# A transformer block in fp32 on one core: both column pairs of the output projection by seven products for eight

## The chip, the cores and the metric

The kernel runs on one core of a Trainium2 chip. The metric is the device time of one execution in microseconds. Its engines work in parallel and wait for each other on semaphores: TensorE (PE, with its weight loads PEld), VectorE (DVE), ScalarE (ACT), GpSimd (POOL) and SyncE (SP), which here issues most of the loads. POOL issues the other DMAs.

## The reference

One residual block over 512 tokens of width 2048, eight stick-breaking heads and eight latent-attention heads, 128 wide each. Cut to what matters here:

```python
h = rms_norm(x, pre_norm_w); proj = h @ w_in
o_a = stick_breaking_attention(sb_q, sb_k, sb_v)            # 8 heads x 128
o_b = chunk_causal_softmax_attention(q_mla, k_mla, v_mla)   # 8 heads x 128
mixed = concatenate([o_a * silu(sb_gate), o_b * silu(mla_gate)])   # 512 x 2048
y = mixed @ w_out                                           # 2048 x 2048
return x + rms_norm(y, post_norm_w)
```

## The kernel before

Every fp32 product is made of three matmuls: each operand is split into a high part (a cast on ScalarE) and a low part (a subtract on VectorE, `split`), and `mm3` adds hi x hi, hi x lo and lo x hi. So each weight tile of 128x1024 (`raw`, loaded by SP) passes ScalarE (`whi`) and VectorE (`wlo`) before TensorE reads it; four raw and three split tiles are in flight.

TensorE never runs attention alone. A generator, `filler()`, yields steps of three matmuls of the big projections in a fixed order: the latent projection, the gates, then for each stick-breaking head q, k and its gate (v of four heads at once, ahead of heads 0 and 4), and last the output projection. The attention code takes such steps between its own matmuls with `fill(n)`, and `need(key)` runs steps until a projection is done. The latent heads come first; the loop over the eight stick-breaking heads h follows, and what is left of the filler, which is the output projection, runs at the end.

A head's result (`mix`, 128 features x 512 tokens) is put into DRAM (`mixed`). For the output projection the kernel loads it again (`mx`) and splits it.

The 2048 output columns are four groups of 512. Groups 0 and 1 go the plain way (`out_group`): 16 feature chunks x 4 token blocks x 3 matmuls each. Groups 2 and 3 are one pair in `last_columns`: features in two halves, tokens in two halves, columns in two halves make a 2x2 block product, which is done with seven half-size products (A11, S1, S2, S3, A22, S4, A12) instead of eight. Its operands are sums of blocks: sums of weights (`w_sums`) and sums of mixed (s1, s2 and s4, `first_sums`; s3, `late_sums`). The weights' sums are made during the heads: `load_weight_parts(j)` loads four 128x512 pieces by POOL into "wsum" tiles, `weight_sums(j)` subtracts on VectorE and stores the results to DRAM by POOL, and the products load them as weights. Each product is 4 weight tiles x 2 chunks x 2 token blocks x 3 matmuls. Sums of the products are added on VectorE (`s1`, `s15`), `sum_piece` makes `y`, its sum of squares and the weighted `y`. The last product is done token block by token block (`kept` weights), and `residual` ends each block.

Tiles come from tagged pools, and a tile waits until its slot is free: "qrt" has 8 slots, "mv" 4, "tr" 4, "g" 48. Instructions marked `keep_in_program_order` keep their order on an engine; the others are placed by the scheduler. The matmuls, SP's loads and the wsum subtracts are marked.

Of the kernel before, what the change touches and what calls it, by code (L numbers as in the profile page):

```python
# [19 lines left out]
P = 128  # L20
S = 512
# [36 lines left out]
def block(ctx: ExitStack, tc: tile.TileContext, a: dict):  # L58
# [317 lines left out]

    order = list(range(H, 2 * H)) + list(range(H))
    msplit = []
    last_mixed = {}

    def split_mixed():
        n = len(msplit)
        if n == 2 * H:
            return
        i = order[n]
        tag = "qrt" if n < 4 else "g"
        hi, lo = g(f"mxh{i}", F32R, tag), g(f"mxl{i}", F32R, tag)
        if i == H - 1:
            mx = last_mixed[0]
        else:  # L390
            mx = g("mx", tag="mv")
            pool.dma_start(out=mx, in_=mixed[i])
        split(hi, lo, mx)
        msplit.append((hi, lo))

    def out_mm(ps, b, c, wh, wl):
        mh, ml = msplit[c]
        mm3(ps, tokens(mh, b), tokens(ml, b), wh, wl, c == 0, c == 15)

    ssy = [const.tile([P, 5], F32, name=f"ssy{b}") for b in range(NB)]  # L400
    ypw = [{} for _ in range(NB)]
    y_tags = iter(["q4"] * 4 + ["row"] * 6 + ["gt"] * 2 + ["g"] * 5)
# [30 lines left out]
    def out_group(gi):  # L433
        banks = [bank(f"y{b}") for b in range(NB)]
        for i in range(8):
            wh, wl = weights(a["w_o"][gi, i], 1024)
            if i == 0:
                for _ in range(4):
                    split_mixed()
            at = 8 * gi + i - 6  # L440
            if 0 <= at + 1 < H:
                load_pair(at + 1)
            if 0 <= at < H:
                first_sums(at)
            for j in range(2):
                s_ = slice(j * S, (j + 1) * S)
                split_mixed()
                for b in range(NB):
                    out_mm(banks[b], b, i * 2 + j, wh[:, s_], wl[:, s_])
                    yield  # L450
        pw = post_weight(gi)
        for b in range(NB):
            out_piece(b, gi * S, banks[b], pw)

# [3 lines left out]
    sums = {}  # L458
    w_sums = [dram.tile([4, P, 1024], F32, name=f"w_sums{n}") for n in range(4)]

    w_parts = {}

    def load_weight_parts(j):
        i, c = j // 2, slice((j % 2) * S, (j % 2 + 1) * S)
        w_parts[j] = []
        for gi, k in ((2, 0), (3, 0), (3, 4), (2, 4)):
            t = g("wsum", tag="qrt")
            tc.keep_in_program_order(pool.dma_start(out=t, in_=a["w_o"][gi, k + i][:, c]))
            w_parts[j].append(t)

    def weight_sums(j):

        i, c = j // 2, slice((j % 2) * S, (j % 2 + 1) * S)
        b11, b12, b22, b21 = w_parts.pop(j)
        for n, (out, x, y) in ((0, (b11, b12, b11)), (2, (b12, b22, b12)), (1, (b22, b22, b11)), (3, (b21, b21, b22))):
            tc.keep_in_program_order(dve.tensor_tensor(out=out, in0=x, in1=y, op=ALU.subtract))
            tc.keep_in_program_order(pool.dma_start(out=w_sums[n][i][:, c], in_=out))

    def mixed_again(n):
        t = g("mx", tag="mv")  # L480
        pool.dma_start(out=t, in_=mixed[order[n]])
        return t

    pairs = {}

    def load_pair(j):
        pairs[j] = mixed_again(j), mixed_again(j + 8)

    def first_sums(j):

        x, y = pairs.pop(j)
        t, s4 = g("st", tag="tr"), g("st4", tag="tr")[:, :HALF]
# [4 lines left out]
        h12, l12, hl4 = g("s12h", F32R), g("s12l", F32R), g("s4", F32R)  # L497
        split(h12, l12, t)
# [514 lines left out]
```

## Time and profile before

| | |
|---|---|
| median of 3 runs | 852.88 us (852.85 to 853.16) |
| the profiled execution | 851.63 us, its span 849.9 us |
| mean granted clock of TensorE, share of full | 0.998 |
| matmuls in the profile | 4050 |
| busy: PE, PEld, DVE, ACT, POOL | 98%, 82%, 57%, 43%, 11% of the span |
| moved by DMA | 126.84 MB |

The profile is of one execution; the span runs from its first instruction to its last. Busy time of an engine is a mean over stretches of different kinds, so stretches are read apart. A row of a timeline gives the start, the length, the engine, the line, output<-inputs, and in brackets how long the engine idled before and what ended it.

### The profile page before, as it was taken

To read this page: it belongs to the slowest core of one execution; us is meant where nothing else is said; L and a number is where in the kernel's file an instruction comes from. 1 tells how busy PE (TensorE), PEld (TensorE's weight loads), DVE (VectorE), ACT (ScalarE), POOL (GpSimd) and SP (SyncE) were. 2 spreads that over 40 slices of the span, in tenths; PEclk is the share of its full clock that TensorE was granted. 3 is DMA by queue.
4 is the path that set the end of the run, shared out by engine and by line. 5 is a ranking of instruction groups with operands and counts; after the bars stand their busy time and mean duration, and the time that the engine had idled before them with its cause. 6 is when DMAs were issued, how large, how long until landed. Compare 5 with 4: busy or idle time off the path is not lost.

```text
span 849.9 us, 10987 instructions
## 1 busy us (share of the span) xinstructions
PE 834.2 (98%) x4050; PEld 700.0 (82%) x4050; DVE 484.5 (57%) x866; ACT 361.6 (43%) x620; POOL 90.2 (11%) x189
## 2 busy tenths in 40 slices
PE   8999999999999999999999999999999999999995
PEld 5889988888888888888888888888878888888884
DVE  5676765556665533647374623555574768435876
ACT  7742655545555323334242413333342535324641
POOL 1000000000000040111111010111120122100001
PEclk9999999999999999999999999999999999999999
DMA  9823222222221164434434342425362556525984
GB/s 333 342 81 106 100 81 81 81 94 81 81 90 65 63 223 161 146 99 164 161 124 154 131 140 97 145 91 199 131 222 98 179 176 222 162 99 182 324 305 155
DMA packets 41909, 126.84 MB, mean 149 GB/s; under 512 B 5808, under 2 KB 6080, under 8 KB 41856
## 3 DMA queue, kind: packets, MB, share of 16 engines
q1 hardware_dynamic: 29952, 88.62, 30.0%
q0 software_dynamic: 10608, 35.42, 12.6%
q10 hardware_dynamic: 1296, 2.11, 0.7%
q8 instruction: 32, 0.52, 0.3%
q14 instruction: 21, 0.17, 0.1%
HBM read 109.34 MB, written 16.78 MB: 148 GB/s over the span
## 4 chain that ended last, share of the span: by engine, by line
PE 87%; DMA 4%; DVE 3%; issue 3%; ACT 1%; POOL 1%; SPq 0%; DVEq 0%; POOLq 0%; ACTq 0%
PE gps L122 19%; PE v L122 10%; PE qp L122 10%; PE kp L122 9%; PE y L122 6%; PE cq L122 4%; PE av L122 4%; PE mz L122 3%; DMA mx<-mixed 3%; PE mqp L122 3%; PE sx L122 3%; PE sz L122 3%; PE ckv L122 2%; PE sv L122 2%; PE tp L125 2%
## 5 line engine op out<-in xcount | busy, mean ns | idle before, releaser
L99 DVE TENSOR_TENSOR wlo<-raw,whi 128x1024 fp32r<-128x1024 f32 (+2 forms) x137 | 163.2, 1191 | 138.6 <-ACT whi L96 137.1
L96 ACT CAST whi<-raw 128x1024 fp32r<-128x1024 f32 (+2 forms) x137 | 140.6, 1026 | 212.5 <-PE v L122 43.5
L122 PE MATMUL gps<-hh,whi 128*128 128x512 f32 x256 | 102.0, 398 | 0.0
L122 PE MATMUL gps<-hl,whi 128*128 128x512 f32 x256 | 100.1, 391 | 0.0
L122 PE MATMUL gps<-hh,wlo 128*128 128x512 f32 x256 | 99.9, 390 | 0.0
L122 PEld LDWEIGHTS gps<-hh,wlo 128*128 128x128 f32 x256 | 48.1, 188 | 10.6
L99 DVE TENSOR_TENSOR tl<-tp,th 128x512 fp32r<-128x512 f32 (+1 forms) x64 | 31.1, 486 | 42.4 <-ACT th L96 42.0
L96 ACT CAST th<-tp 128x512 fp32r<-128x512 f32 (+1 forms) x64 | 27.1, 424 | 66.2 <-PE tp L125 66.0
L122 PEld LDWEIGHTS gps<-hl,whi 128*128 128x128 f32 x256 | 48.3, 189 | 7.6
L122 PEld LDWEIGHTS gps<-hh,whi 128*128 128x128 f32 x256 | 48.2, 188 | 7.6
L122 PE MATMUL qp<-hh,whi 128*128 128x512 f32 x128 | 52.1, 407 | 0.0
L122 PE MATMUL v<-whi,hh 128*128 128x512 f32 x128 | 50.9, 397 | 0.0
L122 PE MATMUL y<-whi,mxh 128*128 128x512 f32 x128 | 50.3, 393 | 0.2 <-DVE y L416 0.2
L122 PE MATMUL qp<-hh,wlo 128*128 128x512 f32 x128 | 50.1, 391 | 0.0
L122 PE MATMUL qp<-hl,whi 128*128 128x512 f32 x128 | 50.0, 391 | 0.0
L122 PE MATMUL v<-whi,hl 128*128 128x512 f32 x128 | 49.9, 390 | 0.0
L122 PE MATMUL v<-wlo,hh 128*128 128x512 f32 x128 | 49.9, 390 | 0.0
L122 PE MATMUL y<-whi,mxl 128*128 128x512 f32 x128 | 49.9, 390 | 0.0
L122 PE MATMUL y<-wlo,mxh 128*128 128x512 f32 x128 | 49.9, 389 | 0.0
L122 PE MATMUL kp<-hh,whi 128*128 128x512 f32 x128 | 49.8, 389 | 0.0
L122 PE MATMUL kp<-hl,whi 128*128 128x512 f32 x128 | 49.8, 389 | 0.0
L122 PE MATMUL kp<-hh,wlo 128*128 128x512 f32 x128 | 49.8, 389 | 0.0
(296 smaller groups left out, 1790.6 us busy)
## 6 DMA issues: line engine op xcount, KB each, us to landing
raw<-in_w_t SPq DMA_DIRECT2D x64, 512.0 KB, 3.3
raw<-in_w_o SPq DMA_DIRECT2D x24, 512.0 KB, 3.3
mx<-mixed POOLq DMA_DIRECT2D x39, 256.0 KB, 3.5
raw<-in_w_v SPq DMA_DIRECT2D x16, 512.0 KB, 3.2
wsum<-in_w_o POOLq DMA_DIRECT2D x32, 256.0 KB, 5.2
w_sums<-wsum POOLq DMA_DIRECT2D x32, 256.0 KB, 2.6
raw<-w_sums SPq DMA_DIRECT2D x16, 512.0 KB, 3.4
xs<-in_x SPq DMA_DIRECT2D x16, 256.0 KB, 6.3
```

The costliest lines, as they stand in the source:

```text
L96: i = act.copy(out=hi, in_=src)
L99: dve.tensor_tensor(out=lo, in0=src, in1=hi.bitcast(F32), op=ALU.subtract)
L122: tc.keep_in_program_order(pe.matmul(out=out, lhsT=lhsT, rhs=rhs, start=start, stop=stop, **kw))
L125: tc.keep_in_program_order(pe.transpose(out, in_, identity))
```

## The change

Both column pairs now go by seven products: `out_columns(u)` for u = 0 (groups 0, 1) and u = 1 (groups 2, 3), in the order A11, S3, S1, S2, S4, A22, A12. `out_group`, `split_mixed`, `first_sums` and `late_sums` are gone.

The weights' sums are made for both pairs, 64 loads and 64 stores instead of 32 and 32. `w_todo` says which eighths belong to which head: two to heads 0 and 4, one to heads 1, 2, 3 and 5. The loads of a head's first eighth (eight at once) are issued in the head before; the sums of pair 0 come before the head's scores, those of pair 1 after them.

The mixed operands' sums are made once for both pairs. `head_sums` makes s1, s2 and s4 behind every head and stores them to DRAM. `latent_parts` loads and splits the latent halves with s3 in place (k1), four in head 6 and four ahead of head 7's scores. `other_parts` loads s12, s4 and the stick-breaking halves (k2) beside the first pair's products A11, S3, S1, S2 and S4, three loads ahead, through the four "mv" slots. The second pair finds all of them split already.

Pinned splits keep their subtract in program order too. Scores of heads 0 to 6 have `fill(6)` ahead, not `fill(4)`. In the tail the second piece instead of the third goes by ScalarE and POOL.

```diff
     def split(hi, lo, src, scale=None, pin=False):
         if scale is None:
             i = act.copy(out=hi, in_=src)
+            j = dve.tensor_tensor(out=lo, in0=src, in1=hi.bitcast(F32), op=ALU.subtract)
             if pin:
                 tc.keep_in_program_order(i)
-            dve.tensor_tensor(out=lo, in0=src, in1=hi.bitcast(F32), op=ALU.subtract)
+                tc.keep_in_program_order(j)
         else:
...
+    w_sums = [[dram.tile([4, P, 1024], F32, name=f"w_sums{u}_{n}") for n in range(4)] for u in range(2)]
+    a_sums = [(dram.tile([P, S], F32, name=f"s12_{j}"), dram.tile([P, HALF], F32, name=f"s4_{j}")) for j in range(H)]
-    def load_weight_parts(j):
+    def load_weight_parts(u, j):
...
+        for gi, k in ((0, 0), (1, 0), (1, 4), (0, 4)):
             t = g("wsum", tag="qrt")
-            tc.keep_in_program_order(pool.dma_start(out=t, in_=a["w_o"][gi, k + i][:, c]))
...
-    def weight_sums(j):
+            tc.keep_in_program_order(pool.dma_start(out=t, in_=a["w_o"][2 * u + gi, k + i][:, c]))
+            w_parts[u, j].append(t)
+    def weight_sums(u, j):
...
-        b11, b12, b22, b21 = w_parts.pop(j)
+        b11, b12, b22, b21 = w_parts.pop((u, j))
         for n, (out, x, y) in ((0, (b11, b12, b11)), (2, (b12, b22, b12)), (1, (b22, b22, b11)), (3, (b21, b21, b22))):
             tc.keep_in_program_order(dve.tensor_tensor(out=out, in0=x, in1=y, op=ALU.subtract))
-            tc.keep_in_program_order(pool.dma_start(out=w_sums[n][i][:, c], in_=out))
-
-    def mixed_again(n):
-        t = g("mx", tag="mv")
-        pool.dma_start(out=t, in_=mixed[order[n]])
+            tc.keep_in_program_order(pool.dma_start(out=w_sums[u][n][i][:, c], in_=out))
+    def from_dram(src, w=S):
+        t = g("mx", tag="mv")[:, :w]
+        pool.dma_start(out=t, in_=src)
         return t
...
+    def head_sums(h, x, y):
+        t, s4 = g("st", tag="mv"), g("st4", tag="mv")[:, :HALF]
         s1, s2 = t[:, :HALF], t[:, HALF:]
         dve.tensor_tensor(out=s1, in0=x[:, HALF:], in1=y[:, HALF:], op=ALU.add)
         dve.tensor_tensor(out=s2, in0=s1, in1=x[:, :HALF], op=ALU.subtract)
         dve.tensor_tensor(out=s4, in0=y[:, :HALF], in1=s2, op=ALU.subtract)
+        pool.dma_start(out=a_sums[h][0], in_=t)
+        pool.dma_start(out=a_sums[h][1], in_=s4)
+    k1, s12, k2, s4s = [], [], [], []
+    def latent_parts(js, tag, steps=2):
+        xs = []
+        for j in js:
+            x = from_dram(mixed[H + j])
+            xs.append(x)
+        for x in xs:
+            fill(steps)
+            tc.keep_in_program_order(dve.tensor_tensor(out=x[:, HALF:], in0=x[:, :HALF], in1=x[:, HALF:], op=ALU.subtract))
+            hi, lo = g("k1h", F32R, tag), g("k1l", F32R, tag)
+            split(hi, lo, x, pin=True)
+            k1.append((hi, lo))
+    def other_parts():
+        srcs = [(a_sums[j][0], S) for j in range(H)] + [(a_sums[j][1], HALF) for j in range(H)] + [(mixed[j], S) for j in range(H)]
+        ahead = [from_dram(*srcs[n]) for n in range(3)]
+        for n in range(3 * H):
+            x = ahead.pop(0)
+            if H <= n < 2 * H:
+                hl4 = g("s4", F32R)
+                split(hl4[:, :HALF], hl4[:, HALF:], x, pin=True)
+                s4s.append(hl4)
+            else:
+                hi, lo = g("kh", F32R), g("kl", F32R)
+                split(hi, lo, x, pin=True)
+                (s12 if n < H else k2).append((hi, lo))
+            if n + 3 < 3 * H:
+                ahead.append(from_dram(*srcs[n + 3]))
+            if n < H or n >= 2 * H or n % 2:
+                yield
...
+    def out_columns(u):
+        w11, w21, w22 = ([a["w_o"][2 * u + gi, k + i] for i in range(4)] for gi, k in ((0, 0), (0, 4), (1, 4)))
+        t1, t2, t3, t4 = w_sums[u]
+        at = (2 * u * S, (2 * u + 1) * S)
+        parts = other_parts() if u == 0 else iter(())
         x = [bank("sx") for _ in range(2)]
+        yield from product(x, "A11", w11, True, False, parts)
         s1 = [g("s1", tag="t") for _ in range(2)]
         s15 = [g("s15", tag="t") for _ in range(2)]
         for r in range(2):
             act.copy(out=s1[r], in_=x[r])
+        v = [bank("sv") for _ in range(2)]
+        yield from product(v, "S3", t3, True, False, parts)
         z = [zbank("sz") for _ in range(2)]
+        beside = parts if u == 0 else keep_weights()
+        yield from product(z, "S1", t1, True, True, beside)
         for r in range(2):
             dve.tensor_tensor(out=s15[r], in0=z[r], in1=s1[r], op=ALU.add)
         y = [tbank("sy") for _ in range(2)]
+        yield from product(y, "S2", t2, True, True, beside)
         for r in range(2):
             dve.tensor_tensor(out=s1[r], in0=y[r], in1=s1[r], op=ALU.add)
             dve.tensor_tensor(out=s15[r], in0=y[r], in1=s15[r], op=ALU.add)
+        pws = [post_weight(2 * u), post_weight(2 * u + 1)]
         junk = g("junk", tag="tr")
         for r in range(2):
+            sum_piece(2 + r, at[1], v[r], s15[r], pws[1], junk)
+        z = [zbank("sz") for _ in range(2)]
+        yield from product(z, "S4", w22, True, True, parts if u == 0 else load_x(2))
         for r in range(2):
+            sum_piece(r, at[1], z[r], s15[r], pws[1], junk)
+        yield from product(v, "A22", t4, False, True, iter(()) if u == 0 else load_x(0))
         for r in range(2):
+            sum_piece(2 + r, at[0], v[r], s1[r], pws[0], junk)
+        if u == 0:
+            yield from product(x, "A12", w21, False, True)
+            for r in range(2):
+                out_piece(r, at[0], x[r], pws[0], junk)
+            return
         for b in (2, 3):
             residual(b)
         for b in (0, 1):
             for j in range(8):
                 mm3(x[b], *factor("A12", j, b), *kept[j], False, j == 7, skip_group_check=True)
                 yield
+            out_piece(b, at[0], x[b], pws[0], junk)
             residual(b, b == 1)
...
-            if tail and i == 2:
+            if tail and i == 1:
...
-        for gi in range(2):
-            yield from out_group(gi)
-        yield from last_columns()
+        for u in range(2):
+            yield from out_columns(u)
...
@@ -917,17 +881,30 @@
         fill(max(0, 4 * NK + NK * (h + 2) - taken[0]))
 
-    load_weight_parts(H - 1)
+    def load_parts(j):
+        for u in range(2):
+            load_weight_parts(u, j)
+    w_todo = {0: [0, 1], 1: [2], 2: [3], 3: [4], 4: [5, 6], 5: [7]}
+    load_parts(0)
     for h in range(H):
-        if h == 0:
-            fill(8)
-            weight_sums(H - 1)
+        late = None
+        for n, j in enumerate(w_todo.get(h, ())):
+            if n:
+                weight_sums(1, late)
+                load_parts(j)
+                fill(30)
+            else:
+                fill(10)
+            weight_sums(0, j)
+            late = j
+        if h == H - 1:
+            latent_parts(range(4, 8), "g")
         kh, kl = need("k", h)
         qh, ql = need("q", h)
-        fill(4)
+        fill(6 if h < H - 1 else 4)
         rows = row_tiles("beta")
-        if h < H - 1:
-            load_weight_parts(h)
+        x = from_dram(mixed[H + h])
         for b in range(NB):
             n = (b + 1) * P
             w = max(n, 256)
@@ -941,17 +918,20 @@
                                    initial=1.0, op0=ALU.mult, op1=ALU.add)
             dve.tensor_tensor(out=beta[:, :n - 1], in0=beta[:, :n - 1], in1=prod[:, 1:n], op=ALU.mult)
             fill((1, 3, 3, 7)[b])
-        if h < H - 1:
-            weight_sums(h)
+        if late is not None:
+            weight_sums(1, late)
+        if h == H - 2:
+            latent_parts(range(4), "qrt", 0)
         cur = Weighted(rows, need("v", h // 4), (h % 4) * P)
         for j in range(NB):
             cur.turn(j)
             fill(3)
             cur.add(j)
+        for j in w_todo.get(h + 1, ())[:1]:
+            load_parts(j)
         out = cur.finish(need("gate", h))
-        if h == H - 1:
-            last_mixed[0] = out
         put_aside(h, out)
+        head_sums(h, x, out)
```

Three places on VectorE show what moves. The first is in head 0, while TensorE runs v of heads 0 to 3; `wlo` is a weight tile's low part, `wsum` a weights' sum, `vl_0` the low part of v that empties the bank of its first token block. Before:

```order
L99 TENSOR_TENSOR wlo<-raw,whi 128x1024
L476 TENSOR_TENSOR wsum<-wsum 128x512 x4
L99 TENSOR_TENSOR wlo<-raw,whi 128x1024 x3
L102 SCALAR_TENSOR_TENSOR vl_0_3357<-v_0_2907,rstd,vh_0_3356 128x512
L102 SCALAR_TENSOR_TENSOR vl_1_3361<-v_1_2908,rstd,vh_1_3360 128x512
```

and now:

```order
L97 TENSOR_TENSOR wlo<-raw,whi 128x1024
L430 TENSOR_TENSOR wsum<-wsum 128x512 x5
L97 TENSOR_TENSOR wlo<-raw,whi 128x1024
L430 TENSOR_TENSOR wsum<-wsum 128x512 x3
L97 TENSOR_TENSOR wlo<-raw,whi 128x1024
L430 TENSOR_TENSOR wsum<-wsum 128x512 x3
L97 TENSOR_TENSOR wlo<-raw,whi 128x1024
L430 TENSOR_TENSOR wsum<-wsum 128x512
L103 SCALAR_TENSOR_TENSOR vl_0_3409<-v_0_2927,rstd,vh_0_3408 128x512
L103 SCALAR_TENSOR_TENSOR vl_1_3413<-v_1_2928,rstd,vh_1_3412 128x512
```

Twelve weights' sums instead of four stand ahead of `vl_0`, with the weight tiles between them.

The second is from the end of head 6 to the scores of head 7. `kr` is k scaled from its bank, `kl` its low part, `k1l` and `mxl` are low parts of mixed, L458 is s3, `st` are s1 and s2. Before:

```order
L790 TENSOR_TENSOR mix<-av,gt 128x512
L99 TENSOR_TENSOR wlo<-raw,whi 128x1024
L99 TENSOR_TENSOR ql<-qp,qh 128x512
L99 TENSOR_TENSOR mxl_6051<-mx,mxh_6050 128x512
L99 TENSOR_TENSOR mxl_6057<-mx,mxh_6056 128x512
L99 TENSOR_TENSOR wlo<-raw,whi 128x1024
L99 TENSOR_TENSOR mxl_6075<-mx,mxh_6074 128x512
L99 TENSOR_TENSOR mxl_6102<-mx,mxh_6101 128x512
L371 TENSOR_TENSOR kr<-kp,rstd_bc 128x512
L99 TENSOR_TENSOR wlo<-raw,whi 128x1024
L99 TENSOR_TENSOR kl<-kr,kh 128x512
```

and now:

```order
L443 TENSOR_TENSOR st<-st,mx 128x256
L444 TENSOR_TENSOR st_6103<-mix,st 128x256
L97 TENSOR_TENSOR wlo<-raw,whi 128x1024
L458 TENSOR_TENSOR mx<-mx 128x256
L97 TENSOR_TENSOR k1l<-mx,k1h 128x512
L458 TENSOR_TENSOR mx<-mx 128x256 x2
L97 TENSOR_TENSOR k1l<-mx,k1h 128x512
L458 TENSOR_TENSOR mx<-mx 128x256
L372 TENSOR_TENSOR kr<-kp,rstd_bc 128x512
L97 TENSOR_TENSOR wlo<-raw,whi 128x1024
L97 TENSOR_TENSOR k1l<-mx,k1h 128x512
L97 TENSOR_TENSOR kl<-kr,kh 128x512
```

Four s3, two k1l and the three sums of head 6's own result now stand ahead of `kr`, and two more k1l around `kl`.

The third is the end of product S2 in the last pair. L592/L593 before and L554/L555 now add the product to `s1` and `s15`, L400 makes y from a finished product, L402 weights it, `wol` is the low part of a kept weight. Before:

```order
L99 TENSOR_TENSOR wlo<-raw,whi 128x1024
L592 TENSOR_TENSOR s_6932<-sy,s_6932 128x512
L593 TENSOR_TENSOR s_6934<-sy,s_6934 128x512
L592 TENSOR_TENSOR s_6933<-sy,s_6933 128x512
L593 TENSOR_TENSOR s_6935<-sy,s_6935 128x512
L99 TENSOR_TENSOR wlo<-raw,whi 128x1024
L99 TENSOR_TENSOR wol<-wk,woh 128x512
L99 TENSOR_TENSOR wlo<-raw,whi 128x1024 x2
```

and now:

```order
L97 TENSOR_TENSOR wlo<-raw,whi 128x1024
L554 TENSOR_TENSOR s_7135<-sy,s_7135 128x512
L555 TENSOR_TENSOR s_7137<-sy,s_7137 128x512
L554 TENSOR_TENSOR s_7136<-sy,s_7136 128x512
L555 TENSOR_TENSOR s_7138<-sy,s_7138 128x512
L400 TENSOR_TENSOR y_7422<-sv,s_7137 128x512
L400 TENSOR_TENSOR y_7426<-sv,s_7138 128x512
L97 TENSOR_TENSOR wlo<-raw,whi 128x1024
L402 TENSOR_TENSOR y_7422<-y_7422,pw 128x512
L402 TENSOR_TENSOR y_7426<-y_7426,pw 128x512
L97 TENSOR_TENSOR wlo<-raw,whi 128x1024 x2
```

The two L400 rows now follow right behind the four adds, ahead of the next weight tile's `wlo`, and each `wlo` alternates with a `wol`.

## Rows read from the trace of the kernel before

**Rows 1.** The page: busy time, share and instructions of each engine.
```profile
...
PE 834.2 (98%) x4050; PEld 700.0 (82%) x4050; DVE 484.5 (57%) x866; ACT 361.6 (43%) x620; POOL 90.2 (11%) x189
...
```

**Rows 2.** Stretches: busy time (x instructions) of each engine, granted clock, DMA share, GB/s.
```profile
...
304.14:489.30 185.16, 185.16 (x864) 154.53 (x863) 97.23 (x142) 63.42 (x95) 26.00 (x53) 1.00 0.44 153
489.30:620.00 130.70, 130.70 (x600) 108.82 (x600) 60.07 (x83) 42.46 (x61) 14.36 (x29) 1.00 0.41 139
...
841.07:849.90 8.83, 0.00 (x0) 0.00 (x0) 3.77 (x4) 1.41 (x3) 2.47 (x3) 0.77 0.44 155
...
```

**Rows 3.** What TensorE waits for after 600 us: total, times, longest.
```profile
...
PE z L122 <- ACT kh L96: 1.3, 1, 1.3
PE sv L122 <- DVE y L423: 0.4, 1, 0.4
PE z L122 <- DVE kl L99: 0.3, 1, 0.3
PE av L122 <- DVE tl L99: 0.3, 1, 0.3
PE y L122 <- DVE y L416: 0.2, 1, 0.2
```

**Rows 4.** The chain that ended last, after 715 us: start, length, what.
```profile
...
720.39 43.85 PE y L122 x192
...
786.00 10.88 PE sy L122 x48
...
```

**Rows 5.** VectorE, 303 to 331 us: start, length, line, operation, idle before.
```profile
...
311.80 2.87 DVE L476 TENSOR_TENSOR wsum<-wsum 128x512 f32<-128x512 f32 x4 [3.24 <-DMA wsum<-in_w_o]
...
326.69 2.11 DVE L102 SCALAR_TENSOR_TENSOR vl<-v,rstd,vh 128x512 fp32r<-128x512 f32 x3 [1.81 <-ACT vh L101]
...
```

**Rows 6.** POOL in the same stretch.
```profile
...
314.96 0.54 POOL L477 DMA_DIRECT2D w_sums<-wsum  x1 [0.19 <-issue]
315.50 2.17 POOL L468 DMA_DIRECT2D wsum<-in_w_o  x4
```

**Rows 7.** The page: DMA issues, KB each, median us from issue to landing.
```profile
...
mx<-mixed POOLq DMA_DIRECT2D x39, 256.0 KB, 3.5
...
wsum<-in_w_o POOLq DMA_DIRECT2D x32, 256.0 KB, 5.2
w_sums<-wsum POOLq DMA_DIRECT2D x32, 256.0 KB, 2.6
...
```

**Rows 8.** DMAs issued from 314 to 322 us, in the same form.
```profile
...
wsum<-in_w_o POOLq DMA_DIRECT2D x4, 256.0 KB, 7.1
...
```

**Rows 9.** Tile wsum: duration (min/median/max ns); all its DMAs to landing.
```profile
...
L468 POOL DMA_DIRECT2D wsum<-in_w_o x32: 546/550/565, 306.2 to 612.0; - x32
...
DMA to landing us min/median/max: 2.2/4.0/7.5
```

**Rows 10.** Tile mx: its DMAs to landing.
```profile
...
DMA to landing us min/median/max: 2.8/3.5/6.2
```

**Rows 11.** The chain that ended last, 300 to 352 us.
```profile
...
327.97 10.88 PE qp L122 x48
...
```

**Rows 12.** VectorE in head 1, from the end of its k.
```profile
...
349.77 0.69 DVE L371 TENSOR_TENSOR kr<-kp,rstd_bc 128x512 f32<-128x512 f32 x1 [3.35 <-PE kp L122]
...
375.96 0.69 DVE L790 TENSOR_TENSOR mix<-av,gt 128x512 f32<-128x512 f32 x1 [1.77 <-PE av L122]
...
387.55 0.69 DVE L371 TENSOR_TENSOR kr<-kp,rstd_bc 128x512 f32<-128x512 f32 x1 [3.31 <-PE kp L122]
...
```

**Rows 13.** VectorE at the ends of products S1 and S2.
```profile
...
785.80 1.29 DVE L586 TENSOR_TENSOR s<-sz,s 128x512 f32<-128x512 f32 x2 [0.17 <-issue]
...
797.88 0.68 DVE L592 TENSOR_TENSOR s<-sy,s 128x512 f32<-128x512 f32 x1
...
799.67 0.68 DVE L593 TENSOR_TENSOR s<-sy,s 128x512 f32<-128x512 f32 x1
800.27 1.21 DVE L99 TENSOR_TENSOR wlo<-raw,whi 128x1024 fp32r<-128x1024 f32 x1
...
```

More of the change, by code (lines that the diff above doesn't have):

```diff
@@ L374, in sb_keys @@
         return kh, kl
[L377 to L398, printed above, removed]
     ssy = [const.tile([P, 5], F32, name=f"ssy{b}") for b in range(NB)]
     ypw = [{} for _ in range(NB)]
-    y_tags = iter(["q4"] * 4 + ["row"] * 6 + ["gt"] * 2 + ["g"] * 5)
+    y_tags = iter(["q4"] * 4 + ["row"] * 6 + ["gt"] * 2 + ["g"] * 4)
     def square_sum(b, ps, junk):
@@ L431, in post_weight @@
         return pw
[L433 to L453, printed above, removed]
@@ L457, in block @@
     HALF = S // 2
-    sums = {}
-    w_sums = [dram.tile([4, P, 1024], F32, name=f"w_sums{n}") for n in range(4)]
+    w_sums = [[dram.tile([4, P, 1024], F32, name=f"w_sums{u}_{n}") for n in range(4)] for u in range(2)]
+    a_sums = [(dram.tile([P, S], F32, name=f"s12_{j}"), dram.tile([P, HALF], F32, name=f"s4_{j}")) for j in range(H)]
     w_parts = {}
-    def load_weight_parts(j):
+    def load_weight_parts(u, j):
         i, c = j // 2, slice((j % 2) * S, (j % 2 + 1) * S)
-        w_parts[j] = []
-        for gi, k in ((2, 0), (3, 0), (3, 4), (2, 4)):
+        w_parts[u, j] = []
+        for gi, k in ((0, 0), (1, 0), (1, 4), (0, 4)):
@@ L527, in keep_weights @@
                 raws.append(loaded(j + 2))
-            hi, lo = g("woh", F32R), g("wol", F32R)
-            split(hi, lo, raws.pop(0))
+            tag = ("qrt", "g")[j % 2]
+            hi, lo = g("woh", F32R, tag), g("wol", F32R, tag)
+            split(hi, lo, raws.pop(0), pin=True)
             kept.append((hi, lo))
@@ L533, in block, with load_x @@
     x_rows = {}
-    def load_x(b0, tag):
+    def load_x(b0):
         for b in (b0, b0 + 1):
@@ L544, in load_x @@
                     yield
-    def both(*gens):
-        while True:
-            for x in gens:
-                next(x, None)
-            yield
     def factor(which, j, r):
         lo_, hi_ = slice(r * P, (r + 1) * P), slice(HALF + r * P, HALF + (r + 1) * P)
-        if which in ("S1", "S2"):
-            c = lo_ if which == "S1" else hi_
-            return sums[j][0][:, c], sums[j][1][:, c]
         if which == "S4":
-            return sums[j][2][:, lo_], sums[j][2][:, hi_]
-        k, c = {"A11": (0, lo_), "S3": (0, hi_), "A12": (8, lo_), "A22": (8, hi_)}[which]
-        return msplit[j + k][0][:, c], msplit[j + k][1][:, c]
+            return s4s[j][:, lo_], s4s[j][:, hi_]
+        of, c = {"A11": (k1, lo_), "S3": (k1, hi_), "S1": (s12, lo_), "S2": (s12, hi_), "A12": (k2, lo_), "A22": (k2, hi_)}[which]
+        return of[j][0][:, c], of[j][1][:, c]
     def product(banks, which, srcs, start, stop, beside=iter(())):
@@ L587, in last_columns @@
         y = [tbank("sy") for _ in range(2)]
-        keeping = keep_weights()
-        yield from product(y, "S2", w_sums[1], True, True)
-        next(keeping)
+        yield from product(y, "S2", t2, True, True, beside)
         for r in range(2):
```

39 lines of the change are left out of this document (1 added, 38 removed).

## The prediction

> **What bounds the kernel now.** I read the page first: TensorE is busy 98% of the span [rows 1], so the next question is where it is not. The table by stretches answers it: from 304 to 489 us and from 489 to 620 us its busy time equals the length of the stretch, at the full clock (1.00), while VectorE is busy for 97 of the first 185 us [rows 2]. There another engine matters only if a wait for it reaches TensorE. After 600 us the list of what TensorE waits for has five entries, 2.5 us together [rows 3]. The last 8.83 us hold no matmul [rows 2]; this tail has the same operations in both kernels (the piece that goes to ScalarE is the second instead of the third), so I leave it as it is.
>
> What does a matmul of the output projection cost? In the chain that ended last, the 192 of the second plain column group take 43.85 us, 0.2 of it a wait [rows 3, 4], and a product of 48 takes 10.88 us, 0.2267 each [rows 4]. So TensorE runs at one pace in both forms, and the change pays by having fewer matmuls, less each new wait.
>
> **The change, part by part.**
>
> *1. Fewer matmuls.* Two plain column groups are 2 x 16 x 4 x 3 = 384 matmuls, seven products 7 x 48 = 336, of the same shape. 48 fewer are one product: **-10.88 us** [rows 4].
>
> *2. The old waits.* Of the five, 1.9 (z for kh and kl, av for tl) came where casts of mixed operands stood ahead of head 7's keys; 0.4 where A22 followed S3 on the same banks, between which S4 now lies; 0.2 where the second plain group waited for the first one's bank, and there is none now. All go: **-2.5** [rows 3]. What stands in head 7 instead is costed under 4.
>
> *3. Weight sums in head 0.* Before, four wsum subtracts stand ahead of v0's end; now twelve do (first order rows of the change). Their second eight loads use the eight "qrt" slots again, so they wait for eight stores. Before, the four subtracts began at 311.80, 0.72 apart [rows 5], and the fourth store was issued at 314.96 [rows 6]. With eight and a weight tile's wlo between them (1.2), the last store goes out and lands enough for the loads to start near 318.7; the second load, which the first subtract needs too, is issued near 319.2. How long does it take? The median of such loads is 5.2 [rows 7], four asked in a row took 7.1 [rows 8], the extremes are 2.2 and 7.5 [rows 9]. With 5.0: three sums 324.2 to 326.3, wlo to 327.5, a fourth sum to 328.1, vl_0 to 328.8. The next projection takes vl_0's bank at 327.97 [rows 11]; vl was there at 326.69 before [rows 5]. So a wait of 0.9; with 7.1 it is 3.0, with 4 none. I take **+1.5** (0 to 3.0), between the median and the four in a row, since now eight are asked.
>
> *4. Head 6 to head 7.* Four loads of k1's operands are asked behind two new stores on POOL, and their subtracts stand ahead of head 7's kr on VectorE (second order rows). I count from the end of k in head 6 (kr starts at once); the period is 387.55 - 349.77 = 37.78, and mix is at 375.96 - 349.77 = +26.2 [rows 12]. In head 6 the first latent casts stand in the scores' chain and two more filler steps lie ahead, so mix comes near +29.5. Three short adds follow; the stores are issued at +30.9 and +31.45, two loads at +32.0 and +32.6, and the other two, which need the slots that the stores free 2.6 later [rows 7], at +33.5 and +34.05. With a landing of 3.5 [rows 7] the last is there at +37.55. Two short subtracts of 0.42 and a k1l of 0.68 stand between it and kr, which then starts at +39.4 instead of +37.8; wlo, k1l and kl behind it end at +42.4. The scores begin some 15 matmuls after k's end, 15 x 0.2267 = 3.4, and read kl one later: +41.4. So **+1.0**; with the shortest and longest landing, 2.8 and 6.2 [rows 10], 0.2 to 3.7. Head 7's transposed halves queue behind more casts than before; by the old wait for tl [rows 3] that is **+0.3** (0 to 1).
>
> *5. First pair, end of S2.* VectorE has four adds, two y, a kl and a wlo ahead of the fourth tile of S4: about 8.6 us of work against 8.4 of cover, **+0.3** (0 to 0.5).
>
> *6. Second pair, end of S2.* Before, two weight tiles were split ahead there: the adds ran from 797.88, one each 0.60, the next wlo stood at 800.27, and TensorE had no wait [rows 13, 3]. Now a wol is cast for each tile of S1 and S2, only one tile is ahead when S2 ends, and VectorE has four adds and both L400 rows before the wlo that S4's 13th matmul reads (third order rows). The adds may begin 0.2 before the product's end, as S1's did at 785.80 against 786.00 [rows 4, 13]. Six at 0.60, a wlo of 1.22, 0.05 to start: -0.2 + 3.6 + 1.22 + 0.05 = 4.67 after the end, while the tile ahead gives 13 x 0.2267 = 2.95. **+1.7** (1.5 to 2.0). This order is fixed by the program, so it is the surest wait of all.
>
> **Costed at nothing, and by what cover.** POOL issues 81 more DMAs, 81 x 0.55 = 45 us [rows 9]; it is busy for 26 of 185 us [rows 2]. Thirty-two more subtracts of 0.68 and twelve more wlo of 1.2 are 36 us of VectorE, spread over stretches of which the first alone has 88 free [rows 2]. In heads 1 to 5 the first four sums stand between the last tl and mix: covered if their loads land in time, which is rival (c). The second four, after beta, end at +5.3 beside the scores, and two more filler steps ahead of these (2 x 3 x 0.2267 = 1.4 us) cover them. In S1 of the first pair two s4 loads are asked in each 2.72 us through four "mv" slots; at 3.5 us of landing the margin is 1.4. Without that cover, at landings of 6.2 to 7.1, the four slots turn once in about 8.5 us, which is 4.25 per tile against 2.72: 6.1 behind over four tiles, less the 2.8 of a tile ahead, **3.3**.
>
> **The sum.** -10.88 - 2.5 + 1.5 + 1.0 + 0.3 + 0.3 + 1.7 = **-8.6**. The profiled execution took 851.63, so it would take 843.0; the median of the runs is 852.88, 1.25 above it, so I forecast a median of **844.3 us**. All lower ends together give -11.7 (841.2); all upper ends, S1's 3.3 among them, near 0.
>
> **The rivals.**
>
> *(a) The transfers land early.* Terms 3 and 4 fall to 0 and 0.2, so -8.6 - 1.5 - 0.8 = -10.9: **842.0 us**. For it stand the medians of mx and w_sums, 3.5 and 2.6 [rows 7]; against it the 7.1 of four loads in a row [rows 8]. The Trainium skill, DMA: Bandwidth & Descriptors, section Anatomy of one DMA — SWDGE (gpsimd) path, gives a transfer as 2.0 us plus its bytes over 436e3, an estimate of 2.6 us for 256 KB. By that rule this rival would hold; the trace agrees for the stores and shows twice as much and more for wsum's loads.
>
> *(b) Operands from DRAM come late.* Landings of 6 us and more in the first pair's S1 (+3.0 beside term 5) and in head 7 (+1.5): -8.6 + 4.5 = -4.1, **848.8 us**. For it: the longest mx landing is 6.2 already [rows 10]. Against it: that was one of 39, and the median is 3.5.
>
> *(c) The other side: the sums come late in every head.* VectorE stands at the first wsum subtract until two loads have landed. Behind it, ahead of kr, it has wlo, ql, mix, three more sums, three short adds and a wlo, 1.2 + 0.7 + 0.7 + 2.0 + 1.3 + 1.2 = 7.1. With kr due at +37.8 the sums must begin by +30.6. The second load is asked at +23.9, so the cover lasts to a landing of 6.7 us, and the added filler gives the scores 2.0 more: 8.7. Past that each microsecond is one of TensorE in five heads, and the gain is gone at 8.7 + 8.6/5 = 10.4. At 12 us it is 5 x 3.3 = 16.5, net +7.9: **860.8 us**. For it: eight loads are asked where four took 7.1 [rows 8]. Against it: 7.5 is the longest seen [rows 9]. POOL's issue shows no delay by VectorE's two-input subtracts, 546 to 565 ns throughout [rows 9]. The Trainium skill, SBUF — State Buffer, section SBUF: two separate sides, says that VectorE can keep GpSimd from writing a DMA's descriptors, so that 620 ns alone became some 3100; put on top of 5.2 that is an estimate of 7.7, which speaks against the change but stays within the cover; no run here shows it yet.
>
> *(d) The new waits eat the gain.* All upper ends together, near 853.
>
> **Chances.** The forecast (842.5 to 846.5) 0.54, (a) 0.15, (b) 0.19: all three are faster by more than 0.2%, 1.7 us, which is about what a measurement of this kernel can tell from no change. (c) 0.07, (d) or a mild (c) 0.05. So faster 0.88, same 0.05, slower 0.07. The range, 841.0 to 849.0, goes from all lower ends to (b).
>
> **What would show it.** 48 matmuls fewer (1). Among TensorE's waits: qp for vl near 328 (3); z for kl in head 7 (4); sz for whi or wlo three microseconds into the second pair's S4, with four adds and two L400 rows ahead of it (6); and none of the five old ones (2). The forecast is wrong if z or qp waits in heads 1 to 5 behind wsum (c), if S1 of the first pair waits for a kl from s12 or s4 (b), or if the clock of a stretch after 304 us is below 1.00.

## The result and the profile after

The changed kernel takes 857.77 us (median of 9 runs, 854.19 to 861.1); the kernel before, 852.85 (9 runs, 850.74 to 854.55). The ratio is 1.0056, 95% interval [1.0036, 1.0075]: slower by about half a percent, where 1.0% faster was forecast. The profiled execution took 856.84 us with a span of 855.1, against 851.63 and 849.9.

First the page of the changed kernel, the line that answers to [rows 1] and the DMA issues of [rows 7].

```profile
PE 827.4 (97%) x4002; PEld 692.5 (81%) x4002; DVE 524.2 (61%) x914; ACT 371.0 (43%) x626; POOL 134.1 (16%) x270
...
wsum<-in_w_o POOLq DMA_DIRECT2D x64, 256.0 KB, 5.3
w_sums<-wsum POOLq DMA_DIRECT2D x64, 256.0 KB, 5.2
...
mx<-mixed POOLq DMA_DIRECT2D x24, 256.0 KB, 4.2
```

TensorE has its 48 matmuls fewer, yet the span is longer: it stands still more. The median landing (from a DMA's issue until it has arrived) of a wsum load is what it was; that of a w_sums store has doubled. What TensorE waits for from 300 us on (total, times, longest), the view of [rows 3]:

```profile
PE qp L123 <- DVE vl L103: 6.0, 1, 6.0
PE sz L123 <- DVE wlo L97: 2.8, 3, 1.3
PE z L123 <- ACT kh L96: 1.5, 1, 1.5
PE z L123 <- DVE kl L97: 1.3, 1, 1.3
PE z L123 <- ACT beta L916: 0.5, 1, 0.5
PE sz L123 <- ACT whi L96: 0.5, 1, 0.5
PE v L123 <- DVE gt L345: 0.4, 1, 0.4
```

Here qp is the q projection, z the scores, v the value projection and sz the bank of S1 and S4. The five old waits are gone, and 13.0 us of new ones stand in their place; the first is the longest. Where the clock was granted in full is in the table by stretches (busy times, then the granted clock, DMA share and GB/s):

```profile
13.58:51.70 38.12, 38.01 (x161) 31.29 (x162) 22.10 (x54) 24.45 (x52) 1.05 (x1) 0.96 0.77 291
304.14:335.66 31.52, 25.49 (x115) 20.81 (x113) 14.17 (x19) 7.89 (x9) 15.56 (x29) 0.94 0.88 296
335.66:348.21 12.55, 12.55 (x49) 10.30 (x50) 4.28 (x5) 1.25 (x2) 0.11 (x1) 0.88 0.50 158
348.21:359.09 10.88, 10.88 (x49) 9.01 (x49) 3.05 (x3) 2.59 (x4) 0.00 (x0) 1.00 0.29 96
658.50:684.65 26.15, 23.39 (x105) 19.03 (x105) 18.35 (x32) 11.27 (x20) 7.07 (x13) 1.00 0.63 206
```

Third row: the q projection behind the long wait took 12.55 us for its 48 matmuls at a mean clock of 0.88, where it took 10.88 before [rows 11]. First row: a slow stretch in the first 52 us, where both kernels run the same instructions; it comes in some executions and not in others (1.00 in six of the nine kernels below), so I do not count this 1.7 us as the change's.

The ledger of the two profiled executions, from the starts of the same matmuls in both traces (us, after minus before):

| stretch | lost or gained |
|---|---|
| first 52 us, slow clock | +1.7 |
| wait of qp for vl_0: q starts at 335.66, before at 327.97, less the 1.7 above | +6.0 |
| q projection of head 0, slow clock: 12.55 - 10.88 | +1.7 |
| z for beta in head 0, v for gt in head 4 | +1.4 |
| the old waits in head 6 | -2.7 |
| head 7: scores 3.3, transposes 0.3 | +3.6 |
| output projection, to the last matmul | -7.1 |
| tail | +0.7 |
| sum (855.1 - 849.9 = 5.2) | +5.3 |

The output projection's -7.1 is -10.9 for the product, -1.1 for the old waits and four new delays: 1.8 in S1, 0.2 in S2 and 1.3 in S4 of the first pair, 1.6 in S4 of the last (from a product's first matmul to the next product's, less 10.88). Each is somewhat longer than the idle time in the list of waits. In the tail, four residual rows of another token block (844.87 to 847.60) stand on VectorE ahead of the last block's, whose three rows now start 3.7 us behind the last matmul's start instead of 2.1.

VectorE and POOL in head 0 of the changed kernel, to set beside [rows 5, 6]:

```profile
317.03 0.69 DVE L430 TENSOR_TENSOR wsum<-wsum 128x512 f32<-128x512 f32 x1 [1.80 <-DMA wsum<-in_w_o]
...
331.06 2.14 DVE L430 TENSOR_TENSOR wsum<-wsum 128x512 f32<-128x512 f32 x3 [9.01 <-DMA wsum<-in_w_o]
...
334.26 0.68 DVE L430 TENSOR_TENSOR wsum<-wsum 128x512 f32<-128x512 f32 x1
334.86 2.06 DVE L103 SCALAR_TENSOR_TENSOR vl<-v,rstd,vh 128x512 fp32r<-128x512 f32 x3
```

```profile
321.21 0.54 POOL L431 DMA_DIRECT2D w_sums<-wsum  x1 [0.19 <-issue]
321.74 2.17 POOL L422 DMA_DIRECT2D wsum<-in_w_o  x4
324.25 0.55 POOL L422 DMA_DIRECT2D wsum<-in_w_o  x1 [0.34 <-DMA w_sums<-wsum]
326.32 0.55 POOL L422 DMA_DIRECT2D wsum<-in_w_o  x1 [1.52 <-DMA w_sums<-wsum]
```

VectorE idles 9.01 us for the second eighth's loads, with vl_0 behind them. The four loads that its next four sums read are asked at 321.74, right behind the eighth store in POOL's order and without a wait of POOL. The last two rows do wait for stores, but they load pair 1's parts, whose sums come after vl_0. The DMAs issued from 321.5 to 324 us landed late, as the issue list of that stretch says:

```profile
wsum<-in_w_o POOLq DMA_DIRECT2D x4, 256.0 KB, 8.6
raw<-in_w_t SPq DMA_DIRECT2D x1, 512.0 KB, 8.7
w_sums<-wsum POOLq DMA_DIRECT2D x1, 256.0 KB, 6.1
```

POOL and VectorE from head 6 to head 7, where term 4 has its place:

```profile
664.77 1.08 POOL L435 DMA_DIRECT2D mx<-mixed  x2 [0.86 <-DMA s<-st]
```

```profile
670.67 0.43 DVE L458 TENSOR_TENSOR mx<-mx 128x256 f32<-128x256 f32 x1 [2.48 <-DMA mx<-mixed]
...
671.95 0.69 DVE L372 TENSOR_TENSOR kr<-kp,rstd_bc 128x512 f32<-128x512 f32 x1
```

And before S1 of the first pair, where loads again wait for stores and VectorE for what they bring:

```profile
704.03 2.17 POOL L435 DMA_DIRECT2D mx<-s  x4 [2.36 <-DMA s<-st]
```

```profile
711.29 0.69 DVE L97 TENSOR_TENSOR kl<-mx,kh 128x512 fp32r<-128x512 f32 x1 [4.35 <-ACT kh L96]
```

### The profile page after: what moved, and what is told of

The parts are those of the page before. It is cut to its first block, busy times and chain, and to the rows that moved or that the text cites. A ratio compares the mean times of both kernels' runs of the same rounds, so it can differ in the third digit from the quotient of the medians.

```text
span 855.1 us, 11124 instructions
## 1 busy us (share of the span) xinstructions
PE 827.4 (97%) x4002; PEld 692.5 (81%) x4002; DVE 524.2 (61%) x914; ACT 371.0 (43%) x626; POOL 134.1 (16%) x270
## 4 chain that ended last, share of the span: by engine, by line
PE 48%; DVE 5%; DMA 3%; issue 3%; ACT 1%; POOL 1%; DVEq 0%; POOLq 0%; ACTq 0%
PE qp L123 10%; PE kp L123 9%; PE gps L123 8%; PE v L123 5%; PE sx L123 4%; PE sv L123 4%; PE sz L123 3%; PE av L123 2%; PE z L123 2%; PE sy L123 1%; DVE xr L597 1%; DMA mx<-mixed 1%; PE tp L126 1%; DMA raw<-in_w_o 1%; DVE wlo L97 1%
## 5 line engine op out<-in xcount | busy, mean ns | idle before, releaser
L96 ACT CAST whi<-raw 128x1024 fp32r<-128x1024 f32 (+2 forms) x149 | 153.2, 1028 | 249.3 <-issue 55.3
L97 DVE TENSOR_TENSOR wlo<-raw,whi 128x1024 fp32r<-128x1024 f32 (+2 forms) x149 | 177.7, 1194 | 108.0 <-ACT whi L96 107.5
L430 DVE TENSOR_TENSOR wsum<-wsum 128x512 f32<-128x512 f32 x64 | 44.1, 689 | 23.1 <-DMA wsum<-in_w_o 22.1
L431 POOL DMA_DIRECT2D w_sums<-wsum x64 | 34.4, 540 | 97.7 <-DVE wsum L430 92.7
L422 POOL DMA_DIRECT2D wsum<-in_w_o x64 | 34.7, 548 | 10.0 <-DMA w_sums<-wsum 7.8
```

The source lines that it names most:

```text
L97: j = dve.tensor_tensor(out=lo, in0=src, in1=hi.bitcast(F32), op=ALU.subtract)
L431: tc.keep_in_program_order(pool.dma_start(out=w_sums[u][n][i][:, c], in_=out))
```

## The experiments

My theory: each wait has a place of its own in an engine's order, and the slow q projection is a consequence of the long wait. The rival: the added traffic and VectorE's added work fill these engines, so a wait undone in one place comes back in another.

Experiments 1 to 5, 8 and 9 are one execution each; the kernel before took 851.34 us beside 1 to 4, 851.73 (median of 7) beside 5 to 7 and 852.48 beside 8 and 9. Times of the changed kernel lie up to 8 us apart (854.19 to 862.16), so what these single runs show is read from their waits, not from their times.

**1. The second eighth behind v.** One number: more filler between head 0's (and head 4's) two eighths.

```diff
                 weight_sums(1, late)
                 load_parts(j)
-                fill(30)
+                fill(46)
```

> Head 0 takes 46 filler steps instead of 30 between the two eighths of the weights' sums, so VectorE has vl_0 ahead of the second eighth's subtracts; the same loads and stores are issued. Theory 1 (qp waits only because late sums stand ahead of vl on VectorE, and the slow matmuls behind that wait come from the wait): the 6.0 us wait of qp for vl is gone, the 1.7 us that the next 48 matmuls took longer are gone too, granted clock 1.00 from 304 to 359 us, the other waits stay (head 7 about 2.8, S4 1.2 and 1.7), time some 7 to 8 us below the changed kernel, near 849 to 850. Theory 2 (the DMA engines are full there, and weight tiles or later work come late whatever the order): at least 3 us of it come back as other waits between 304 and 400 us, time above 853.

It took 849.27 us, span 847.5. VectorE now has vl at 326.75 and the four sums at 330.96; the wait of qp is gone, and the chain shows q at its old place and pace:

```profile
328.03 10.88 PE qp L123 x48
338.91 10.88 PE kp L123 x48
```

So 7.7 us (6.0 and 1.7) hung on the order of a few VectorE rows. The same transfers were made, and the second eighth's loads landed as late as before (median 7.9 us); now nothing stood behind them. Nothing of it came back before 400 us. In head 7, however, the waits grew from 2.8 to 3.6, and the clock of 640 to 700 us was 0.94, where the changed kernel's profile shows 1.00 over its head 7. That the time came out as expected is therefore luck: 7.7 less for the order, 1.6 for a first stretch at full clock and 1.7 in the output projection, 3.4 more in head 7.

**2. The second eighth in free slots.** The loads of head 0's second eighth go to slots that v of heads 4 to 7 uses later, and are asked right behind the first eight.

```diff
     load_parts(0)
+    load_parts(1, "g")
     for h in range(H):
...
-                load_parts(j)
+                if h:
+                    load_parts(j)
```

> The second eighth's eight loads go into eight free slots of another tag and are asked right behind the first eight; VectorE's order keeps all twelve sums ahead of vl_0. If the wait is made by the slots (eight loads that wait for eight stores to land), the loads are there by about 322 us and the qp wait falls from 6.0 to under 1. If it is made by the amount of transfer (16 loads, 8 stores and 4 weight tiles, about 8 MB at some 300 GB/s are 28 us), the last loads still land near 330 and the wait stays above 3 us.

850.14 us, span 848.4, no wait of qp, with VectorE's order as it was. VectorE and POOL there:

```profile
321.76 2.86 DVE L430 TENSOR_TENSOR wsum<-wsum 128x512 f32<-128x512 f32 x4
...
328.14 2.11 DVE L103 SCALAR_TENSOR_TENSOR vl<-v,rstd,vh 128x512 fp32r<-128x512 f32 x3 [1.81 <-ACT vh L102]
```

```profile
317.95 1.20 POOL L422 DMA_DIRECT2D wsum<-in_w_o  x2 [0.39 <-DMA wsum<-in_w_o]
319.53 3.65 POOL L431 DMA_DIRECT2D w_sums<-wsum  x6 [0.38 <-DVE wsum L430]
```

The second eighth's first four sums run with no idle time ahead of vl. What changed is when their loads were asked: from 311.7 to 314.3 us instead of 321.7 to 323.4, ahead of all stores (the first is asked at 319.53) and not behind eight of them. They still took 6.5 to 7.3 us to land, nearly all of it before the first store was asked. So the 6 us came for the most part from the loads' late place in POOL's order, behind eight stores whose sums waited for the first eight loads; a smaller part is the landing, a median of 8.6 instead of 6.6. The edit moves both at once and does not tell them apart further. Experiments 1 and 2 undo two different links of one chain, and each is enough.

**3. Adds behind the second weight tile of S4.**

```diff
+            if then and i == 1:
+                then()
...
-        for r in range(2):
-            dve.tensor_tensor(out=s1[r], in0=y[r], in1=s1[r], op=ALU.add)
-            dve.tensor_tensor(out=s15[r], in0=y[r], in1=s15[r], op=ALU.add)
...
+        def finish_s3():
...
-        yield from product(z, "S4", w22, True, True, parts if u == 0 else load_x(2))
+        yield from product(z, "S4", w22, True, True, parts if u == 0 else load_x(2), finish_s3)
```

> The four adds and the y of S3 are written behind the second weight tile of S4, so in the last pair two adds instead of four adds and two L400 stand ahead of the wlo that S4's 13th matmul needs. Theory 1: -0.2 + 1.2 + 1.22 + 0.05 = 2.3 is less than 2.95, so S4's 1.7 us wait in the last pair is gone; in the first pair only a kl moves ahead, and 1.2 becomes about 0.6. If the wlo is late for another reason (its raw tile or its cast), the 1.7 us stay. The rest as in the changed kernel: qp 6.0, head 7 about 2.8.

855.31 us, span 853.6 (with qp at 6.7 us in this execution). `finish_s3` holds the four adds and then S3's `sum_piece`. S4's waits are gone in both pairs; what sz waits for is one entry, and it is S1's:

```profile
PE sz L123 <- DVE wlo L97: 0.8, 1, 0.8
```

In the last pair the cause is shown: S4 loses 1.6 us in each of the seven traces with the old order and nothing in the three with this one (3, 6 and 7), which lose 0.5 in A22 behind it instead. In the first pair, where I had expected 0.6 to stay, this run does not show it. Experiments 4, 5 and 9 have the old order and lose 0.2 or less there, and in experiment 6, with the new order, a wait of 0.6 is back. The wait follows the moment at which VectorE begins the adds. In the changed kernel that is 1.2 us behind S4's start in the first pair, with VectorE still at a tile's `wlo`, and at the end of S2 in the last pair, where VectorE had stood idle:

```profile
733.70 1.23 DVE L97 TENSOR_TENSOR wlo<-raw,whi 128x1024 fp32r<-128x1024 f32 x1
734.85 0.68 DVE L554 TENSOR_TENSOR s<-sy,s 128x512 f32<-128x512 f32 x1
```

```profile
810.68 0.69 DVE L554 TENSOR_TENSOR s<-sy,s 128x512 f32<-128x512 f32 x1 [2.45 <-PE sy L123]
```

In the four traces with the old order in which the adds begin 1.0 to 1.4 us behind S4's start, S4 loses 1.1 to 1.6; in the three in which they begin before it, 0.2 at most.

**4. The latent halves earlier.**

```diff
-        if h == H - 1:
-            latent_parts(range(4, 8), "g")
...
-        if h == H - 2:
-            latent_parts(range(4), "qrt", 0)
+        if h >= H - 4 and h < H - 1:
+            js = {4: (0, 1), 5: (2, 3), 6: (4, 5, 6, 7)}[h]
+            latent_parts(js, "g" if h < 6 else "qrt", 0)
```

> The latent halves are loaded and split two in head 4, two in head 5 and four in head 6, behind the scores, none ahead of head 7's scores. Theory 1 (loads behind head 6's stores hold kr and kl): the 1.5 and 1.3 us waits of z in head 7 are gone and no new wait of z appears in heads 5 to 7; qp 6.0 stays. Rival (the store and load traffic of head 6, or ScalarE's casts of weight tiles, are what is late): z in head 7 still waits over 1 us.

851.41 us, span 849.7. The waits of z for kh and kl are gone, and heads 5 to 7 have none in their place, only 0.2 of av for tl. S2 of the first pair shows 0.6 that the changed kernel did not have.

**5. Head 7's sums split on the chip.** For the last head, `head_sums` splits s1, s2 and s4 from its tiles instead of storing them, and `other_parts` leaves these two loads out. The tiles of these sums come from the "tr" slots instead of "mv", so the stores and the turn of the "mv" slots go together.

```diff
+        if h == H - 1:
+            hi, lo, hl4 = g("kh", F32R), g("kl", F32R), g("s4", F32R)
+            split(hi, lo, t)
+            split(hl4[:, :HALF], hl4[:, HALF:], s4)
+            last.append(((hi, lo), hl4))
+            return
         pool.dma_start(out=a_sums[h][0], in_=t)
```

> Head 7's own s1, s2 and s4 are split on the chip instead of being stored and loaded again; the rest is the changed kernel. If the S1 waits of the first pair (0.6 and 1.0 us) come from head 7's operands, whose loads stand behind its stores in the four slots (last kl at 711.3 in the changed kernel), both are gone and S1 has no wait over 0.3. If they come from VectorE's or ScalarE's load of work in S1 (tile, kl and s4 splits), about 1 us stays. qp 6.0 and z 2.8 stay as they were.

853.42 us, span 851.7. S1 of the first pair has no wait; S4 of the last pair still loses 1.6, z waits 1.7 and 1.3, qp 5.1. In this execution S4's first-pair wait is missing too. S1's loss is not a fixed size, though: with head 7's round trip in place it was 1.8 in the changed kernel, 1.1 in experiments 8 and 9, 1.4 and 1.2 in 3 and 4, 0.5 in 2 and 0.2 in 1. Why it differs is open.

**6. Three waits undone together, 7. and the fourth.**

> The order of head 0 with 46 steps, S3's y and the adds behind S4's second tile, and the latent halves in heads 4 to 6, all together. If the waits add up one by one: 855.1 - 6.0 - 1.7 - 2.8 - 1.7 - 0.6 = 842.3 of span, or 840.6 where the first stretch keeps its clock, so a time of 842.5 to 844.5 and a ratio to before of 0.988 to 0.990. If the waits only change place (VectorE or DMA are full): above 848, ratio over 0.995.

> The same with head 7's sums split on the chip. If S1's waits belong to head 7's round trip: 1.0 to 1.6 us less than with three, 841 to 843.5 us, ratio 0.986 to 0.989. If not: the same time as with three.

With 1, 3 and 4 together: 841.04 us (840.0 to 841.82, 4 runs), ratio to the kernel before 0.9869 [0.9853, 0.9886]. With 5 as well: 840.78 (839.92 to 841.7), 0.9871 [0.9855, 0.9886], no difference that can be told. Beside them the kernel before took 851.73. The gains add up at least one by one: the span of the profiled run with three, 840.1, is near the 840.6 that was expected where the first stretch keeps its clock, and the medians lie 1.5 us below the 842.5 and 0.2 below the 841 that I had written for them. The rival falls. What TensorE still waits for with all four, from 300 us on:

```profile
PE z L123 <- ACT beta L935: 0.5, 1, 0.5
PE v L123 <- DVE gt L345: 0.4, 1, 0.4
PE sv L123 <- DVE wlo L97: 0.2, 1, 0.2
PE av L123 <- DVE tl L97: 0.2, 1, 0.2
```

Either is a version to keep, some 11 us faster than the kernel before. That this equals the product's 10.9 is a coincidence: by the matmuls' starts of experiment 7, 3.8 us of old waits are gone as well, and 3.3 of small delays are left (0.8 in head 0, 0.6 in head 4, 1.2 in the output projection, 0.7 in the tail). The expectation for the fourth, another 1.0 to 1.6, was wrong: with three undone the trace had no wait in S1 left to remove, only the 0.6 in S4 of the first pair, and the medians show no gain from the fourth.

**8. TensorE kept busy during the wait.** 27 matmuls on operands that are there, into a spare bank, ahead of the q projection of head 0.

```diff
+            if h == 0:
+                busy = zbank("busy")
+                for _ in range(27):
+                    mm(busy, tokens(hh[0], 0), hh[0], True, True)
             done["q", h] = yield from sb_queries(h)
```

> The changed kernel with 27 added matmuls (27 x 0.227 = 6.1 us) into a spare bank, right ahead of the q projection that waits for vl_0; they use operands that are there and their result is not read. If the slow q matmuls (12.55 us for 48 instead of 10.88) come from TensorE standing still during the wait, the 48 take 10.9 at a granted clock of 1.00, and q still starts about 6 to 7 us later than in the kernel before: the time is some 1.7 us below the changed kernel's profiled run, about 855 where the first stretch is slow too, 853.5 where not. If something else in that stretch (the traffic, the operands' reading) makes them slow, they still take over 12 us.

855.48 us, span 853.5. The chain and the stretches of this kernel:

```profile
327.38 6.12 PE busy L123 x27
333.50 10.88 PE qp L123 x48
344.38 1.81 PE kp L123 x8
```

```profile
333.34:344.38 11.04, 11.04 (x50) 9.17 (x49) 2.41 (x3) 1.25 (x2) 0.00 (x0) 1.00 0.42 144
```

The q projection runs at its old pace, at 1.00. The slow 1.7 us come from TensorE standing still, not from the traffic, which at 0.90 of the DMA engines up to q's start was no less (0.88 in the changed kernel); during q it was 0.42 against 0.50, but in experiment 9 q is slower still at 0.46. The time is only 1.4 below the changed kernel's profiled run, though the first 52 us were at full clock here: head 7's waits brought a slow stretch (0.91 from 640 to 680 us), which they had not there.

**9. The changed kernel again.**

> The changed kernel once more, to see which of its waits and slow stretches come in every execution: qp near 6 us with a clock of 0.94 behind it, z 2.8 to 3.6 in head 7, S4 1.2 and 1.7. The nine timed runs lie between 854.2 and 861.1 with mean clocks of 0.987 to 0.993; if a second slow stretch explains the higher ones, a lower clock shows behind head 7's wait here or in the first 52 us, and not elsewhere.

862.16 us, span 860.5. Its waits (the three largest), and its stretches:

```profile
PE qp L124 <- DVE vl L104: 6.9, 1, 6.9
PE z L124 <- ACT kh L97: 3.7, 1, 3.7
PE sz L124 <- DVE wlo L98: 2.0, 2, 1.3
```

```profile
336.36:350.25 13.89, 13.89 (x49) 11.27 (x50) 4.28 (x5) 1.24 (x2) 0.12 (x1) 0.79 0.46 142
660.00:700.00 40.00, 35.18 (x154) 28.60 (x153) 26.49 (x42) 18.25 (x30) 8.56 (x17) 0.91 0.53 169
```

Three places come again and are worse: the long wait 6.9, the q projection 13.89 instead of 10.88, head 7's first wait 3.7 with a slow stretch behind it. The first 52 us were slow as well (0.96). In the first pair it differs from what I expected: S1 loses 1.1, S2 1.4, and S4, for which I had written 1.2, nothing; S4 of the last pair loses its 1.6 again. That the higher of the nine timed runs (mean clocks down to 0.987) are of this kind is likely by their clocks, but no trace here shows it.

## Why the prediction was wrong, step by step

- **Term 1** (-10.9) was right: 48 matmuls fewer, and a product without a wait takes 10.88 us from its start to the next one's, as before.
- **Term 2** (-2.5) named waits that did go, but counted only their idle time; by the matmuls' starts they had cost 3.8, 2.7 in head 6 and 1.1 in the output projection. I had put the old waits for kh and kl in head 7; they were in head 6.
- **Term 3** (+1.5) is the step that failed: it cost 6.0, and 1.7 of slow clock behind it, 7.7 in all. The place was right, vl_0 behind the late sums. The link was not quite as written: the four loads that hold vl_0 stood behind the issue of eight stores in POOL's order, and none of them waited for a store to land. Three inputs were off. The last of the eight stores was issued at 321.21, or 319.5 without the slow start, which left the second load 1.4 later than forecast, because VectorE had to wait 1.8 us for the second four loads too. That load was needed at once and let VectorE go on at 331.06, close to the 8.6 of its group, where I took 5.0: some 3.8 more. I read the landing off a median and a group of four among eight loads and four stores; here 16 loads and eight stores were asked from 307.4 to 328.3 us, at a DMA share of 0.88. And the clock was in no term: I took a wait of TensorE to cost its own length.
- **Term 4** (+1.3) measured 3.6. The place and the order were right; the last of the four loads landed 5.3 us behind its issue where I took 3.5, and kr started 3.5 us behind k's end instead of 1.6. The 3.3 of the scores lies within the range of 0.2 to 3.7 that I gave the wait.
- **Term 5** (+0.3) was 1.3. I had the order, but let the adds begin at the end of S2; VectorE began them 1.2 us later, behind what it still had to do, and the tile that came late was S4's third, not its fourth. In the three traces with the old order in which the adds begin before S4's start, nearly nothing is lost, so the forecast's size fits only a VectorE that has caught up. Why it had not is not shown by an experiment of its own.
- **Term 6** (+1.7) was 1.6, in all seven traces with that order. No transfer is in it, and VectorE stands idle ahead of it.
- **Costed at nothing, but not nothing:** S1 of the first pair, 1.8. The prediction gave landings of 3.5 us as its cover and 3.3 as the loss at 6.2 to 7.1; the loads of 704.03 waited for stores of head 7's sums, took some 6.5, and VectorE idled 4.35 us for one kh until 711.29. Experiment 5, without this round trip, has no wait there. Also S2 behind it (0.2), z behind the four sums and a table load in head 0 (0.8), v for gt in head 4 (0.6), and the tail (0.7), which I had called the same in both.
- **Rivals.** (b) had the right kind, operands from DRAM late, at 848.8, but not the place that cost most. (c) did not come: from head 1 to 3 and from head 4 to 6, k ends 37.78 apart as before. (d), all upper ends together, near 853, was nearest, and I had given it with a mild (c) 0.05. Of the prediction's own signs of being wrong, the clock below 1.00 after 304 us showed, and S1's wait in another form: for a weight tile that stood behind a late kl, not for the kl itself. The upper ends were not independent: long landings move terms 3, 4 and S1 together, and this, with no term for the clock, I take to have made the range too narrow.

The Trainium skill, DMA: Bandwidth & Descriptors, section Anatomy of one DMA — SWDGE (gpsimd) path, has a formula that gives an estimate of 2.6 us for 256 KB; here the loads took 8.6 in a full stretch, so the rule would have put term 3 at nothing and missed 7.7 us. The Trainium skill, DMA: Bandwidth & Descriptors, section Latency and other measured facts, says that access to HBM takes 0.2 us on average and 2 us at high load. The trace agrees in direction only: in head 0 the sums' stores landed 2.3 to 3.1 us behind their issue in the kernel before and 5.9 to 6.9 in the changed one.

## What to carry to other kernels

Ask of every wait that a change adds whether a transfer is in it. A wait worked out from an instruction order and durations came out to a tenth where the engine stood idle ahead of it (term 6), and was missed by 1.0 where the engine was behind with other work (term 5). One that ends with a transfer among a dozen others is to be priced at the landing in the fullest stretch seen or beyond, and its neighbours' upper ends are to be added with it. Before counting on free time of an engine, look at which row it would wait behind: here one filler count, a few adds and an earlier load decided between +0.6% and -1.3%, with the same work done.

## What the runs showed of the hardware

A wait of TensorE can cost more than its length. Behind waits of 6.0 and 6.9 us the next 48 matmuls took 12.55 and 13.89 us instead of 10.88, at mean granted clocks of 0.88 and 0.79: some of them ran at the lower of its two levels (1.2 instead of 2.4 GHz), and matmuls started 0.43 apart there instead of 0.227. With 27 matmuls in the wait the clock stayed at 1.00. In head 7, seven traces (the changed kernel twice and experiments 1, 2, 3, 5 and 8) have waits of 2.8 to 4.8 us for kh and kl; from the end of k to the end of the gate behind it, five of them lost 2.1 to 3.2 us on top of the waits' idle time, and two (the changed kernel's first trace and experiment 5) only about 0.5. The price of the same wait so varies from run to run: with 2.8 us of waits the changed kernel's first trace lost about 0.5 more and experiment 8 3.2, at granted clocks of 1.00 (658.50 to 684.65 us) and 0.91 (640 to 680). The Trainium skill, TensorE: Matmul & The Clock Gate, section Part 1: The HAM clock gate (the "warmup" mystery), says that activity releases the throttle; experiment 8 agrees, with the clock at 1.00 where TensorE was given work in the wait.

POOL's issue of a DMA kept its length, 546 to 555 ns for 64 wsum loads, beside 32 more two-input subtracts on VectorE. The Trainium skill, SBUF — State Buffer, section SBUF: two separate sides, warns that a VectorE operation in a two-port mode, such as an fp32 copy, can keep GpSimd from writing descriptors. The operations added here are subtracts of two inputs, and no run shows such a delay at the issue; whether it has a part in the long landings was not tested.
